# Whole projection tiles as 512 sample columns and 128 context columns, the context's halves in one product

## The chip, the cores and the metric

The kernel runs on one core of one Trainium2 chip. The time is device time in microseconds of one execution; 2773.0 us is the median of three runs of the kernel before (2765.32 to 2773.76). One profiled execution, 2764.28 us, gives the trace that is read here.

## The reference

One inference step of four layers, each a token mixer (windowed attention, spatial gating, short convolution, Fourier mixing) followed by a gated convolutional feed-forward part. 128 context tokens and 512 sample tokens go through the same weights. The dense products are nearly all of it:

```
def conv_ffn(h, w_up, conv_w, w_down):
    a = conv3_centred(h @ w_up, conv_w)
    g, u = a[..., :D_FF], a[..., D_FF:]
    return (jax.nn.silu(g) * u) @ w_down
```

with 1024 model columns and D_FF = 2816, in fp32. Before each sub-layer an RMS norm is modulated by shift and scale, and the result is added back through a gate, both from conditioning vectors (`c @ ada_w + ada_b`, other values for context and sample).

## The kernel before, in words

Activations lie with features on partitions and the 640 tokens on the free axis, the context's 128 first (`NP`, then `NS` = 512, `NT` = 640). To keep fp32 accuracy at the speed of fp32r, each operand is held as a high and a low part in fp32r, `[128, 4, 2, 640]` for activations (four feature blocks, high and low, tokens) and `[128, 2, 1024]` for a weight chunk. A product is then three: high x high, high x low, low x high (`mm3`, lines 489 to 491).

An output tile is 128 features x 640 tokens in a pair of PSUM banks (`new_pair`; the pool `pp` has three pairs). A bank holds 512 fp32, so the tile is done in two halves of 320 tokens, placed from column 192 (`PC0`) so that each half lies in one bank. For each k-step of 128 input features and each half, `pe_half` issues the three products: six products of 320 columns in a k-step.

`proj` runs over the output tiles of one weight matrix. A group of three tiles at the start (`lead`) is interleaved by a written plan, since its inputs are still being made; a group of three at the end (`tail`) lets the next norm start on the first half; the tiles between them are whole, one after the other. After a tile's products, `post` evacuates it, `ada.flush()` issues ACT's late accumulations, `W.pump` splits the next weight chunk (ACT casts the high part, L85; DVE, or POOL in places, subtracts for the low part, L86), and `ada.filler` issues one step of the modulation sums of a later layer: on DVE L208, on POOL L213, on ACT L214. The order of every engine is the order of the program.

In the feed-forward part the 44 up tiles of a layer go in three parts (16, 14, 14), each followed by the eight down tiles that sum into the residual (`PARTS`). In an up tile's `post`, ACT writes the middle tap (L612), DVE adds the outer taps for context and sample apart (L614 and L616, twice each), and the gate (L629 on ACT), the product (L636 on POOL, or L621 and L636 on DVE for the last two) and the split of the result (L589, L590) of the tiles before follow. The last three tiles of a part carry no step of the modulation (`quiet=3`). The down part begins with a lead of three tiles, one after the other over the first four k-steps, so it needs all three PSUM pairs; its residual add is L581.

Of the kernel before, what the change touches and what calls it, by code (L numbers as in the profile page):

```python
# [15 lines left out]
KT = 8  # L16
# [6 lines left out]
PC0 = 192  # L23
# [76 lines left out]
class Ada:  # L100
# [225 lines left out]
class Norm:  # L326
# [121 lines left out]

    def rhs(self, k, lo, hi):
        h = self.h[k // 4]  # L450
        return h[:, k % 4, 0, lo:hi], h[:, k % 4, 1, lo:hi]

# [41 lines left out]
def pe_half(g, ps, w, rhs, half, nk=KT, ks=None, at=None):  # L494
    out = ps[:, PC0 + OFF[half]:PC0 + OFF[half] + 320]
    for k in (range(nk) if ks is None else ks):
        rh, rl = rhs(k, OFF[half], OFF[half] + 320)
        c = slice(k * 128, (k + 1) * 128)
        mm3(g.nc, out, w[:, 0, c], w[:, 1, c], rh, rl, k == 0, k == nk - 1)
        if at and k in at:  # L500
            at[k]()


# [4 lines left out]
def proj(g, nm, M, rhs, post, nk=KT, lead=1, split=None, plan=None, hook=None, pre=None, tail=0, norm=None, rate=0.0, m0=0, quiet=0):  # L508
# [21 lines left out]
    while m < M - tail:  # L530
        if pre:
            w, ps = pre.pop(0)
        else:
            w, ps = W.take(), new_pair(g, f"{nm}{m0 + m}")
            pe_half(g, ps, w, rhs, 0, nk)
        for half in (1,):
            pe_half(g, ps, w, rhs, half, nk)
        post(m0 + m, ps, None)
        ada.flush()
        W.pump(g.wpool)  # L540
        ada.filler(rate if m < M - tail - quiet else 0.0)
        m += 1
# [30 lines left out]
def residual(g, l, i, norm=None):  # L573

    nc = g.nc

    def post(m, ps, half):
        lo, hi = (0, NT) if half is None else (OFF[half], OFF[half] + 320)
        gate = g.mod[:, l, i]
        for a, b, v in segs(lo, hi):  # L580
            nc.vector.scalar_tensor_tensor(out=g.x[:, m, a:b], in0=ps[:, PC0 + a:PC0 + b], scalar=gate[:, m, v:v + 1],  # L581
                                           in1=g.x[:, m, a:b], op0=ALU.mult, op1=ALU.add)
        if norm is not None:
            norm.add(m, half)
    return post
# [7 lines left out]
def ffn(g, l, norm, nxt):  # L593
# [10 lines left out]
    for p, (f0, nf) in enumerate(PARTS):  # L604
# [3 lines left out]
        def post(m, ps, half):  # L608
            f, isu = m // 2, m % 2
            col = (f + (NFF if isu else 0)) * 3  # L610
            c = g.tmp.tile([128, 640], F32, tag="tmp", name=f"c{l}_{m}")
            nc.scalar.activation(c, ps[:, PC0:PC0 + NT], AF.Copy, scale=fc[:, col + 1:col + 2])  # L612
            for a, b in ((0, NP), (NP, NT)):
                nc.vector.scalar_tensor_tensor(out=c[:, a + 1:b], in0=ps[:, PC0 + a:PC0 + b - 1], scalar=fc[:, col:col + 1],  # L614
                                               in1=c[:, a + 1:b], op0=ALU.mult, op1=ALU.add)
                nc.vector.scalar_tensor_tensor(out=c[:, a:b - 1], in0=ps[:, PC0 + a + 1:PC0 + b], scalar=fc[:, col + 2:col + 3],  # L616
                                               in1=c[:, a:b - 1], op0=ALU.mult, op1=ALU.add)
# [26 lines left out]

        def grhs(k, lo, hi):
            q = gq[k // 4]
            return q[:, k % 4, 0, lo:hi], q[:, k % 4, 1, lo:hi]

# [24 lines left out]
def attention(g, norm, nxt):  # L673
# [277 lines left out]
    proj(g, "wob", WA, orhs(1), residual(g, 0, 2, nxt), nk=4, rate=g.rate)  # L951
    proj(g, "wo", 3, lambda k, lo, hi: orhs(k // 4)(k % 4, lo, hi), residual(g, 0, 2, nxt), m0=WA, tail=3, norm=nxt, rate=0.0)


def sgu(g, norm, nxt):
# [5 lines left out]
    for q0 in range(0, 4, grp):  # L961
# [90 lines left out]
def shortconv(g, norm, nxt):  # L1052
# [46 lines left out]
def fnet(g, norm, nxt):  # L1099
# [77 lines left out]
def body(ctx, tc, io, depth=DEPTH):  # L1177
# [239 lines left out]
```

## Time and profile before

| what | value |
|---|---|
| median of three runs | 2773.0 us |
| profiled execution, and its span | 2764.28 us, 2762.5 us |
| TensorE products, busy | 2686.8 us, 97% of the span |
| weight loads, busy | 2613.8 us, 95% |
| DVE, ACT, POOL busy | 62%, 38%, 32% |
| DMA, mean | 107 GB/s |

How to read it: records of TensorE's products overlap, so their mean length (309 ns for 320 columns) is not their pace; the pace is read from start to start. DVE's share is a mean over stages that differ widely: in the first three layers' up projections it is near full, in the last layer's it is not.

### The profile page before, as it was taken

The numbers are of one execution on the slowest core, as the hardware profiler recorded it, in microseconds if no ns is written. First come the engines' busy times: TensorE is split into PE (matmuls) and PEld (weight loads), VectorE is DVE, ScalarE is ACT, GpSimd is POOL, SyncE is SP. The second block draws the span as 40 slices with busy tenths as digits, with TensorE's granted clock in tenths as the row PEclk, the third lists the DMA queues.
The fourth block names the chain that finished last, engine by engine and source line by source line (L and its number), as shares of the span: only waits on it lengthen the run. The fifth ranks groups of instructions, "written<-read, shape, count | busy, mean of one in ns | idle before, by whom it ended". The sixth has DMA issues, their size and how long they took to land.

```text
span 2762.5 us, 45506 instructions
## 1 busy us (share of the span) xinstructions
PE 2686.8 (97%) x18950; PEld 2613.8 (95%) x18950; DVE 1721.5 (62%) x2646; ACT 1043.7 (38%) x1672; POOL 878.3 (32%) x449
## 2 busy tenths in 40 slices
PE   8798899999999999999999999999999999999998
PEld 6676799999999999999999999999999999999998
DVE  6344687686964468586876335867678646434344
ACT  4344353343433245343444223534344424223232
POOL 1222153454520027354542001734354213111121
PEclk9999999999999999999999999999999999999999
DMA  6233333434322224333432221434343122221221
GB/s 255 79 100 114 116 128 119 145 131 144 140 75 73 73 81 158 122 136 125 152 107 71 77 77 55 160 115 140 121 153 126 47 69 78 69 83 63 84 70 45
DMA packets 88335, 295.35 MB, mean 107 GB/s; under 512 B 9665, under 2 KB 15553, under 8 KB 88129
## 3 DMA queue, kind: packets, MB, share of 16 engines
q1 hardware_dynamic: 87554, 292.19, 31.1%
q8 instruction: 149, 2.44, 0.3%
q14 instruction: 56, 0.46, 0.0%
q10 hardware_dynamic: 576, 0.26, 0.0%
HBM read 289.53 MB, written 2.88 MB: 106 GB/s over the span
## 4 chain that ended last, share of the span: by engine, by line
PE 85%; issue 7%; DVE 5%; ACT 2%; POOL 1%; DMA 1%; SPq 0%; POOLq 0%; DVEq 0%; ACTq 0%
PE up L489 15%; PE up L491 15%; PE up L490 15%; PE dn L489 6%; PE dn L491 6%; PE dn L490 6%; PE sc L489 2%; PE sc L490 2%; PE sc L491 2%; DVE t L417 1%; PE S L770 1%; PE O L849 1%; POOL w L86 1%; ACT w L85 1%; PE T L826 1%
## 5 line engine op out<-in xcount | busy, mean ns | idle before, releaser
L490 PE MATMUL up<-h,w 128*128 128x320 f32 x2816 | 871.2, 309 | 1.7 <-DVE h L429 1.7
L489 PE MATMUL up<-h,w 128*128 128x320 f32 x2816 | 872.1, 310 | 0.0
L491 PE MATMUL up<-h,w 128*128 128x320 f32 x2816 | 870.9, 309 | 0.0
L490 PEld LDWEIGHTS up<-h,w 128*128 128x128 f32 x2816 | 529.2, 188 | 3.1 <-DVE h L429 2.8
L489 PEld LDWEIGHTS up<-h,w 128*128 128x128 f32 x2816 | 529.2, 188 | 0.3
L491 PEld LDWEIGHTS up<-h,w 128*128 128x128 f32 x2816 | 529.1, 188 | 0.0
L86 DVE TENSOR_TENSOR w<-raw,w 128x1024 fp32r<-128x1024 f32 (+2 forms) x267 | 459.5, 1723 | 103.9 <-ACT w L85 96.1
L86 POOL TENSOR_TENSOR w<-raw,w 128x1024 fp32r<-128x1024 f32 (+2 forms) x94 | 218.6, 2326 | 796.1 <-ACT w L85 665.7
L213 POOL TENSOR_TENSOR adaq<-adaq,cb 128x1024 f32<-128x1024 f32 x138 | 349.7, 2534 | 360.0 <-ACT adaq L214 306.3
L85 ACT CAST w<-raw 128x1024 fp32r<-128x1024 f32 (+2 forms) x361 | 364.2, 1011 | 239.7 <-PE dn L491 162.2
L489 PE MATMUL dn<-g,w 128*128 128x320 f32 x1408 | 436.3, 310 | 0.0
L491 PE MATMUL dn<-g,w 128*128 128x320 f32 x1408 | 435.1, 309 | 0.0
L490 PE MATMUL dn<-g,w 128*128 128x320 f32 x1408 | 435.0, 309 | 0.0
L612 ACT ACTIVATE c<-up,fcv 128x640 f32<-128x640 f32 x176 | 140.1, 796 | 618.0 <-PE up L491 614.2
L614 DVE SCALAR_TENSOR_TENSOR c<-up,fcv,c 128x127 f32<-128x127 f32 x352 | 191.4, 544 | 251.3 <-ACT c L612 250.9
L490 PEld LDWEIGHTS dn<-g,w 128*128 128x128 f32 x1408 | 264.3, 188 | 0.3
L489 PEld LDWEIGHTS dn<-g,w 128*128 128x128 f32 x1408 | 264.3, 188 | 0.3
L491 PEld LDWEIGHTS dn<-g,w 128*128 128x128 f32 x1408 | 264.3, 188 | 0.0
L581 DVE SCALAR_TENSOR_TENSOR x<-dn,mod,x 128x128 f32<-128x128 f32 (+3 forms) x204 | 99.3, 526 | 250.5 <-PE dn L491 250.4
L208 DVE CUSTOM_DVE_ANT_0 adaq<-adaq,cb 128x1024 f32<-128x1024 f32 x138 | 254.5, 1844 | 0.1
L636 POOL TENSOR_TENSOR c<-c,c 128x640 f32<-128x640 f32 x64 | 150.1, 2345 | 180.0 <-DVE c L616 180.0
L616 DVE SCALAR_TENSOR_TENSOR c<-up,fcv,c 128x127 f32<-128x127 f32 x352 | 193.6, 550 | 12.4
(239 smaller groups left out, 3902.5 us busy)
## 6 DMA issues: line engine op xcount, KB each, us to landing
raw<-up SPq DMA_DIRECT2D x176, 512.0 KB, 3.7
adaq<-ada_t SPq DMA_DIRECT2D x138, 512.0 KB, 3.5
raw<-down SPq DMA_DIRECT2D x64, 448.0 KB, 3.6
adar<-ada SPq DMA_DIRECT2D x32, 512.0 KB, 3.5
raw<-down SPq DMA_DIRECT2D x32, 512.0 KB, 3.8
raw<-sc_in SPq DMA_DIRECT2D x24, 512.0 KB, 3.4
ada<-ada SPq DMA_DIRECT2D x16, 512.0 KB, 10.2
raw<-sgu_in SPq DMA_DIRECT2D x16, 512.0 KB, 3.6
```

Of the source, the lines that this page charges most:

```text
L85: nc.scalar.copy(w[:, 0, :n], raw[:, :n])
L86: (nc.gpsimd if pool else nc.vector).tensor_tensor(out=w[:, 1, :n], in0=raw[:, :n], in1=w[:, 0, :n], op=ALU.subtract)
L208: nc.vector.tensor_tensor_reduce(out=p0, in0=t, in1=g.cb[:, 0], scale=1.0, scalar=0.0, op0=ALU.mult, op1=ALU.add, accum_out=acc[:, 0:1])
L213: nc.gpsimd.tensor_tensor(out=p1, in0=t, in1=g.cb[:, 1], op=ALU.mult)
L489: nc.tensor.matmul(out, wh, rh, start=first, stop=False)
L490: nc.tensor.matmul(out, wh, rl, start=False, stop=False)
L491: nc.tensor.matmul(out, wl, rh, start=False, stop=last)
L581: nc.vector.scalar_tensor_tensor(out=g.x[:, m, a:b], in0=ps[:, PC0 + a:PC0 + b], scalar=gate[:, m, v:v + 1], in1=g.x[:, m, a:b], op0=ALU.m ...
L612: nc.scalar.activation(c, ps[:, PC0:PC0 + NT], AF.Copy, scale=fc[:, col + 1:col + 2])
L614: nc.vector.scalar_tensor_tensor(out=c[:, a + 1:b], in0=ps[:, PC0 + a:PC0 + b - 1], scalar=fc[:, col:col + 1], in1=c[:, a + 1:b], op0=ALU. ...
L616: nc.vector.scalar_tensor_tensor(out=c[:, a:b - 1], in0=ps[:, PC0 + a + 1:PC0 + b], scalar=fc[:, col + 2:col + 3], in1=c[:, a:b - 1], op0= ...
L636: eng.tensor_tensor(out=cg, in0=cg, in1=c, op=ALU.mult)
```

## The change

Whole tiles no longer go by halves. `pe_whole` computes, for each k-step, with the high weights the context's high and low parts side by side (one product of 256 columns, into columns 256 to 511 of the pair's first bank), then the sample's high and its low part (512 columns each, the second bank), and with the low weights the sample's high part (512) and the context's high part (128, onto columns 384 to 511). Columns 256 to 383 and 384 to 511 then each hold a part of the context's sum. After the last k-step ACT copies the first of them to a new small tile `ctx` (pool of two) and DVE adds it onto the second, in PSUM. The tile now starts at column 384, which the evacuations read through `g.pc`. Lead and tail tiles, and those that attention interleaves, stay as they were. The scratch output of the fused product and sum L147 moves from a tile of its own into the pool `tmp`.

```diff
+def pe_whole(g, ps, w, rhs, nk=KT):
+    PE = g.nc.tensor
+    for k in range(nk):
+        h = rhs(k)
+        wh, wl = w[:, 0, k * 128:(k + 1) * 128], w[:, 1, k * 128:(k + 1) * 128]
+        first, last = k == 0, k == nk - 1
+        PE.matmul(ps[:, 256:512], wh, h[:, :, 0:NP], start=first, stop=False)
+        PE.matmul(ps[:, 512:1024], wh, h[:, 0, NP:NT], start=first, stop=False)
+        PE.matmul(ps[:, 512:1024], wh, h[:, 1, NP:NT], start=False, stop=False)
+        PE.matmul(ps[:, 512:1024], wl, h[:, 0, NP:NT], start=False, stop=last)
+        PE.matmul(ps[:, 384:512], wl, h[:, 0, 0:NP], start=False, stop=last)
+    t = g.ctx.tile([128, NP], F32, tag="ctx", name="ctx")
+    g.nc.scalar.copy(t, ps[:, 256:384])
+    g.nc.vector.tensor_tensor(out=ps[:, 384:512], in0=ps[:, 384:512], in1=t, op=ALU.add)
...
     while m < M - tail:
         if pre:
             w, ps = pre.pop(0)
+            pe_half(g, ps, w, rhs, 1, nk)
         else:
             w, ps = W.take(), new_pair(g, f"{nm}{m0 + m}")
-            pe_half(g, ps, w, rhs, 0, nk)
-        for half in (1,):
-            pe_half(g, ps, w, rhs, half, nk)
+            pe_whole(g, ps, w, rhs, nk)
+            g.pc = 384
         post(m0 + m, ps, None)
+        g.pc = PC0
         ada.flush()
...
-            nc.scalar.activation(c, ps[:, PC0:PC0 + NT], AF.Copy, scale=fc[:, col + 1:col + 2])
+            nc.scalar.activation(c, ps[:, g.pc:g.pc + NT], AF.Copy, scale=fc[:, col + 1:col + 2])
...
-            V.tensor_tensor_reduce(out=t if v else g.junk, in0=t, in1=g.cb[:, v, c], scale=1.0, scalar=0.0, op0=ALU.mult, op1=ALU.add,
+            V.tensor_tensor_reduce(out=t if v else g.tmp.tile([128, 640], F32, tag="tmp", name=f"junk{self.pos}_{a}")[:, :512], in0=t, in1=g.cb[:, v, c], scale=1.0, scalar=0.0, op0=ALU.mult, op1=ALU.add,
```

Three places in the order of the engines, all at the tile `up_0_9` of the second layer's first part (`h` the normed activations, `w` the weight chunk). TensorE, the first k-steps of the tile, before:

```order
L489 MATMUL up_0_9_9958<-h_1_0_9207,w_9683 128x320
L490 MATMUL up_0_9_9958<-h_1_0_9207,w_9683 128x320
L491 MATMUL up_0_9_9958<-h_1_0_9207,w_9683 128x320
L489 MATMUL up_0_9_9958<-h_1_0_9207,w_9683 128x320
L490 MATMUL up_0_9_9958<-h_1_0_9207,w_9683 128x320
L491 MATMUL up_0_9_9958<-h_1_0_9207,w_9683 128x320
```

and now, from the last product of the tile ahead:

```order
L515 MATMUL up_0_8_9552<-h_1_1_8894,w_9297 128x128
L511 MATMUL up_0_9_9614<-h_1_0_8893,w_9359 128x256
L512 MATMUL up_0_9_9614<-h_1_0_8893,w_9359 128x512
L513 MATMUL up_0_9_9614<-h_1_0_8893,w_9359 128x512
L514 MATMUL up_0_9_9614<-h_1_0_8893,w_9359 128x512
L515 MATMUL up_0_9_9614<-h_1_0_8893,w_9359 128x128
```

Five products stand for six, and a 128-column one stands ahead of each k-step's first. DVE around the same tile, before (`c` is the convolved tile, `adaq` the modulation's block):

```order
L208 ISA adaq_9291,part<-adaq_9291,cb 128x1024
L208 ISA part 128x1
L614 SCALAR_TENSOR_TENSOR c_9_10007<-up_0_9_9958,fcv_9292,c_9_10007 128x127
L616 SCALAR_TENSOR_TENSOR c_9_10007<-up_0_9_9958,fcv_9292,c_9_10007 128x127
L614 SCALAR_TENSOR_TENSOR c_9_10007<-up_0_9_9958,fcv_9292,c_9_10007 128x511
L616 SCALAR_TENSOR_TENSOR c_9_10007<-up_0_9_9958,fcv_9292,c_9_10007 128x511
L86 TENSOR_TENSOR w_10015<-raw_9886,w_10015 128x1024
```

and now (L614 and L616 have become L632 and L634):

```order
L208 ISA adaq_8977,part<-adaq_8977,cb 128x1024
L208 ISA part 128x1
L518 TENSOR_TENSOR up_0_9_9614<-up_0_9_9614,ctx 128x128
L632 SCALAR_TENSOR_TENSOR c_9_9658<-up_0_9_9614,fcv_8978,c_9_9658 128x127
L634 SCALAR_TENSOR_TENSOR c_9_9658<-up_0_9_9614,fcv_8978,c_9_9658 128x127
L632 SCALAR_TENSOR_TENSOR c_9_9658<-up_0_9_9614,fcv_8978,c_9_9658 128x511
L634 SCALAR_TENSOR_TENSOR c_9_9658<-up_0_9_9614,fcv_8978,c_9_9658 128x511
L86 TENSOR_TENSOR w_9666<-raw_9547,w_9666 128x1024
```

The add stands between the step of the tile ahead and this tile's taps. ACT at the same tile, now (L612, the middle tap, has become L630):

```order
L85 CAST w_9606<-raw_9484 128x1024
L517 COPY ctx<-up_0_9_9614 128x128
L630 ACTIVATE c_9_9658<-up_0_9_9614,fcv_8978 128x640
L647 ACTIVATE c_8_9596<-c_8_9596 128x640
L214 ACTIVATE adaq_8977,part<-adaq_8977 128x1024
```

The copy is new, ahead of the middle tap, which reads what the add has written.

## Rows read from the trace of the kernel before

**Rows 1.** The page: busy us of the engines, share of the span, instructions

```profile
PE 2686.8 (97%) x18950; PEld 2613.8 (95%) x18950; DVE 1721.5 (62%) x2646; ACT 1043.7 (38%) x1672; POOL 878.3 (32%) x449
```

**Rows 2.** Timeline, TensorE, up projection (start, length, engine, line, tiles, shapes)

```profile
1086.49 0.31 PE L489 MATMUL up<-h,w 128*128 128x320 f32 x1
...
1114.79 0.31 PE L490 MATMUL up<-h,w 128*128 128x320 f32 x1
```

**Rows 3.** Timeline, TensorE, sgu's value projection

```profile
869.98 0.28 PE L489 MATMUL sv<-w,h 128*128 128x256 f32 x1
...
877.90 0.28 PE L489 MATMUL sv<-w,h 128*128 128x256 f32 x1
```

**Rows 4.** Timeline, TensorE, Fourier mixer

```profile
2218.50 0.39 PE L490 MATMUL f<-dftM,U 128*128 128x512 f32 x1
...
2220.77 0.39 PE L491 MATMUL f<-dftM,U 128*128 128x512 f32 x1
```

**Rows 5.** Timeline, loads and products behind six one-column products, attention's output projection

```profile
341.96 0.19 PEld L489 LDWEIGHTS wo<-O,w 128*128 128x128 f32 x1
341.98 0.39 PE L489 MATMUL wo<-O,w 128*128 128x320 f32 x1
342.07 0.19 PEld L490 LDWEIGHTS wo<-O,w 128*128 128x128 f32 x1
...
342.21 0.31 PE L490 MATMUL wo<-O,w 128*128 128x320 f32 x1
```

**Rows 6.** Windows, up projection (length; PE, PEld, DVE, ACT, POOL busy; clock; DMA)

```profile
1050.00:1120.00 70.00, 70.00 (x479) 70.00 (x479) 62.99 (x73) 33.21 (x49) 37.74 (x18) 1.00 0.39 137
```

**Rows 7.** Timeline, DVE, two step tiles of the same up projection

```profile
1080.55 0.35 DVE L614 SCALAR_TENSOR_TENSOR c<-up,fcv,c 128x127 f32<-128x127 f32 x1
...
1081.97 0.75 DVE L616 SCALAR_TENSOR_TENSOR c<-up,fcv,c 128x511 f32<-128x511 f32 x1
...
1085.60 2.60 DVE L208 CUSTOM_DVE_ANT_0 adaq<-adaq,cb 128x1024 f32<-128x1024 f32 x1
1088.13 0.08 DVE L208 DVE_READ_ACCUMULATOR2_ANT part<- 128x1 f32 x1
...
1090.21 3.02 DVE L86 TENSOR_TENSOR w<-raw,w 128x1024 fp32r<-128x1024 f32 x1
1093.15 1.21 DVE L208 CUSTOM_DVE_ANT_0 adaq<-adaq,cb 128x1024 f32<-128x1024 f32 x1
1094.30 0.08 DVE L208 DVE_READ_ACCUMULATOR2_ANT part<- 128x1 f32 x1
```

**Rows 8.** Timeline, ACT, the middle taps of these tiles

```profile
1079.65 0.80 ACT L612 ACTIVATE c<-up,fcv 128x640 f32<-128x640 f32 x1 [3.64 <-PE up L491]
...
1086.69 0.80 ACT L612 ACTIVATE c<-up,fcv 128x640 f32<-128x640 f32 x1 [3.64 <-PE up L491]
```

**Rows 9.** Timeline, POOL, the same tiles

```profile
1084.56 2.56 POOL L636 TENSOR_TENSOR c<-c,c 128x640 f32<-128x640 f32 x1
...
1089.73 2.42 POOL L213 TENSOR_TENSOR adaq<-adaq,cb 128x1024 f32<-128x1024 f32 x1
```

**Rows 10.** Timeline, DVE, the last tiles of the part, without a step

```profile
1111.24 1.23 DVE L86 TENSOR_TENSOR w<-raw,w 128x1024 fp32r<-128x1024 f32 x1 [0.36 <-ACT w L85]
1115.74 0.35 DVE L614 SCALAR_TENSOR_TENSOR c<-up,fcv,c 128x127 f32<-128x127 f32 x1 [3.28 <-ACT c L612]
...
1120.39 1.23 DVE L86 TENSOR_TENSOR w<-raw,w 128x1024 fp32r<-128x1024 f32 x1
```

**Rows 11.** Timelines, DVE and TensorE, the third down tile behind the last up tile

```profile
1124.21 0.75 DVE L616 SCALAR_TENSOR_TENSOR c<-up,fcv,c 128x511 f32<-128x511 f32 x1
...
1125.21 0.31 PE L489 MATMUL dn<-g,w 128*128 128x320 f32 x1
```

**Rows 12.** Timeline, TensorE, an idle time (in brackets), and the window behind it

```profile
324.39 0.61 PE L489 MATMUL wo<-O,w 128*128 128x320 f32 x1 [2.83 <-DVE x L581]
...
324.13:327.54 3.41, 3.15 (x12) 3.18 (x13) 2.41 (x4) 1.67 (x2) 0.00 (x0) 0.50 0.46 159
```

More of the change, by code (lines that the diff above doesn't have):

```diff
@@ L447, in drain, with rhs @@
             self.low = None
-    def rhs(self, k, lo, hi):
-        h = self.h[k // 4]
-        return h[:, k % 4, 0, lo:hi], h[:, k % 4, 1, lo:hi]
+    def rhs(self, k):
+        return self.h[k // 4][:, k % 4]
     def hook(self, half, k):
@@ L496, in pe_half @@
     for k in (range(nk) if ks is None else ks):
-        rh, rl = rhs(k, OFF[half], OFF[half] + 320)
+        h = rhs(k)[:, :, OFF[half]:OFF[half] + 320]
         c = slice(k * 128, (k + 1) * 128)
-        mm3(g.nc, out, w[:, 0, c], w[:, 1, c], rh, rl, k == 0, k == nk - 1)
+        mm3(g.nc, out, w[:, 0, c], w[:, 1, c], h[:, 0], h[:, 1], k == 0, k == nk - 1)
         if at and k in at:
             at[k]()
+def pe_whole(g, ps, w, rhs, nk=KT):
[12 more added lines that the diff above has]
+    g.nc.vector.tensor_tensor(out=ps[:, 384:512], in0=ps[:, 384:512], in1=t, op=ALU.add)
 def new_pair(g, nm):
@@ L580, in post @@
         for a, b, v in segs(lo, hi):
-            nc.vector.scalar_tensor_tensor(out=g.x[:, m, a:b], in0=ps[:, PC0 + a:PC0 + b], scalar=gate[:, m, v:v + 1],
+            nc.vector.scalar_tensor_tensor(out=g.x[:, m, a:b], in0=ps[:, g.pc + a:g.pc + b], scalar=gate[:, m, v:v + 1],
                                            in1=g.x[:, m, a:b], op0=ALU.mult, op1=ALU.add)
@@ L611, in post @@
             c = g.tmp.tile([128, 640], F32, tag="tmp", name=f"c{l}_{m}")
[L612 removed]
+            nc.scalar.activation(c, ps[:, g.pc:g.pc + NT], AF.Copy, scale=fc[:, col + 1:col + 2])
             for a, b in ((0, NP), (NP, NT)):
[L614 removed]
+                nc.vector.scalar_tensor_tensor(out=c[:, a + 1:b], in0=ps[:, g.pc + a:g.pc + b - 1], scalar=fc[:, col:col + 1],
                                                in1=c[:, a + 1:b], op0=ALU.mult, op1=ALU.add)
[L616 removed]
+                nc.vector.scalar_tensor_tensor(out=c[:, a:b - 1], in0=ps[:, g.pc + a + 1:g.pc + b], scalar=fc[:, col + 2:col + 3],
                                                in1=c[:, a:b - 1], op0=ALU.mult, op1=ALU.add)
@@ L643, in ffn, with grhs @@
         flush()
-        def grhs(k, lo, hi):
-            q = gq[k // 4]
-            return q[:, k % 4, 0, lo:hi], q[:, k % 4, 1, lo:hi]
+        def grhs(k):
+            return gq[k // 4][:, k % 4]
         last = p == len(PARTS) - 1
@@ L724, in post @@
             t = g.tmp.tile([128, 640], F32, tag="tmp", name=f"q{j}")
-            A.copy(t[:, 128:640], ps[:, PC0 + 128:PC0 + 640])
-            A.copy(at.qst[:, j, :128], ps[:, PC0:PC0 + 128])
+            A.copy(t[:, 128:640], ps[:, g.pc + 128:g.pc + 640])
+            A.copy(at.qst[:, j, :128], ps[:, g.pc:g.pc + 128])
             rope_S([(at.qst[:, j, 128:640], 0, 512)], t, f"q{j}")
@@ L729, in post @@
             t = g.tmp.tile([128, 640], F32, tag="tmp", name=f"k{j}")
-            A.copy(t, ps[:, PC0:PC0 + NT])
+            A.copy(t, ps[:, g.pc:g.pc + NT])
             A.dma_start(out=io["new_k"][:, j, :], in_=t[:, :128])
@@ L735, in post @@
             t = g.tmp.tile([128, 640], F32, tag="tmp", name=f"v{j}")
-            A.copy(t, ps[:, PC0:PC0 + NT])
+            A.copy(t, ps[:, g.pc:g.pc + NT])
             A.dma_start(out=io["new_v"][:, j, :], in_=t[:, :128])
@@ L882, in orhs @@
     def orhs(gp):
-        return lambda k, lo, hi: (at.O[gp][:, k, 0, lo:hi], at.O[gp][:, k, 1, lo:hi])
+        return lambda k: at.O[gp][:, k]
     WA = KT - 3
@@ L971, in vmm @@
         def vmm(i, tc, k):
-            hh, hl = norm.rhs(k, tc * 128, (tc + 1) * 128)
+            h = norm.rhs(k)[:, :, tc * 128:(tc + 1) * 128]
+            hh, hl = h[:, 0], h[:, 1]
             w = ws[i][k // 4]
@@ L1044, in sgu, with rhs @@
     proj(g, "su", KT, norm.rhs, post, rate=g.srate)
-    def rhs(k, lo, hi):
-        return oq[k // 4][:, k % 4, 0, lo:hi], oq[k // 4][:, k % 4, 1, lo:hi]
+    def rhs(k):
+        return oq[k // 4][:, k % 4]
     out_proj(g, "sgo", 1, rhs, nxt, lead=3, plan=late_plan(KT, 4), split=0)
@@ L1059, in post @@
         j, kind = m // 3, m % 3
-        pv = ps[:, PC0:PC0 + NT]
+        pv = ps[:, g.pc:g.pc + NT]
         if kind == 0:
@@ L1167, in fnet, with rhs @@
             stage2(k - 1)
-    def rhs(k, lo, hi):
-        return oq[k // 4][:, k % 4, 0, lo:hi], oq[k // 4][:, k % 4, 1, lo:hi]
+    def rhs(k):
+        return oq[k // 4][:, k % 4]
     g.W.cap = len(g.W.chunks)
@@ L1189, in body @@
     g.fcv = pool("fcv", 1)
+    g.ctx = pool("ctx", 2)
     g.quad = pool("quad", 5)
@@ L1231, in body @@
     g.wpool = False
+    g.pc = PC0
     g.rate, g.urate, g.drate, g.srate, g.mix = 1.0, 1.0, 1.0, 0.0, 1
```

9 lines of the change are left out of this document (4 added, 5 removed).

## The prediction

> **What bounds the kernel now.** I read the page first: TensorE is busy 97% of the span and its weight loads 95%, DVE 62% [rows 1]. A busy share of overlapping records is not a pace, so the second view is the timeline of TensorE alone, in stretches without a wait, from start to start. In an up projection 193 starts lie between 1086.49 and 1114.79 us: 146.6 ns for each 320-column product [rows 2]. The sgu products of 256 columns follow each other at 7.92 us / 66 = 120.0 ns [rows 3], those of 512 columns in the Fourier mixer at 2.27 us / 10 = 227 ns [rows 4]. All three lie on one line: 0.4167 ns a column (the 2.4 GHz level) and about 13.3 ns for each product. The reader is to see that columns cost nearly everything, and that one product less is worth 13 ns at most.
>
> The third view is TensorE's loads beside its products where a product is short [rows 5]. Six one-column products stand just ahead. The load for L489 is issued at 341.96, the next load only at 342.07, and L490's product at 342.21, 0.14 to 0.15 after that: in the steady rows a load is issued when the product before it really begins, so L489's product, recorded at 341.98, began at about 342.07. One fp32r load of 128 columns needs 0.11 us and only one is held ahead. Under a 320-column product it is hidden; under a short one it is not.
>
> The fourth view is DVE in the same up stretch. Over 70 us TensorE is never idle, and DVE is busy 62.99 [rows 6]. In a tile that carries a step of the modulation sums (L208) DVE has no room: its L208 ends at 1088.21, 1.5 us after the next tile's L612 began on ACT [rows 7, 8]. So there are two limits here, one almost on top of the other.
>
> **The change part by part.** *Products.* A k-step had six products of 320 columns, now 256, three of 512, and 128: 1920 columns either way, one product less. Whole tiles are: qkv 3, wob 5 (four k-steps each), su 8, the three output projections 2 each, sc 21, up 41 a layer, dn 12 a layer (5 of 8 k-steps, 7 of 7). k-steps: 24 + 20 + 64 + 48 + 168 + 1312 + 356 = 1992, in 255 tiles. The order of TensorE has 1992 rows less.
>
> Before, a k-step takes 6 x 146.6 = 880 ns. After: 120 + 3 x 227 + X, where X is the time from the 128-column product to the next one's start. No row shows such a product in fp32r. From below, the line of rows 2 to 4 gives 53 + 13 = 67 ns, if its successor's load is hidden; from above 111 + 13 = 124 ns, if the fixed part adds to the load. I take 111 ns, the load of rows 5, which is the nearest: a load of the same type behind a product shorter than itself. Then the k-step is 120 + 681 + 111 = 912 ns, 32 ns more, and 1992 x 32 = **+63 us**; the ends are -24 and +89 us. A tile of eight k-steps goes from 7.04 to 7.29 us. Only the last product of a k-step is too short; the 256-column one ahead is not, since 120 ns cover a load.
>
> The Trainium skill has a rule against this choice: "TensorE: Matmul & The Clock Gate", section on weight-path perf modes, says that a fast weight load is on for 128 weights of any type but FP32. By it the load would be hidden, X would be 67 ns and this term -24 us. Rows 5 speak against it for fp32r.
>
> *The sum of the halves.* Each whole tile gains a copy on ACT and an add on DVE, both 128x128 and out of PSUM, ahead of the tile's evacuation. The nearest row for the add is L614's 128x127 with one operand in PSUM, 0.35 us [rows 7]; the copy I put at the same. 255 x 0.35 = 89 us for each engine beside TensorE, which would be free if they were idle. In the up projections the position matters more than the length. ACT's L612 reads the sum, so it now waits for DVE's add, and the add stands in DVE's queue behind the last tile's L86 and L208. Before, L612 ran while DVE was still at that L208: it starts at 1086.69 and DVE ends at 1088.21 [rows 7, 8]. Now DVE does the add, waits for L612 (0.80), then does L614 and L616. Queued behind that waiting instruction are L86 (the low halves of weights taken five tiles later, so no hurry), L208, and the next tile's add, for whose tile three PSUM pairs wait.
>
> Work of a step tile on DVE, from L612's end to the end of L208's read: 1080.45 to 1088.21 = 7.76, and 1087.49 to 1094.38 = 6.89, mean 7.32 us [rows 7, 8]. It is that long because L86 and L208, 1.23 and 1.21 us when alone, take 3.02 and 2.60 when POOL's L213 or L636 runs [rows 7, 9, 10]; POOL's steps hang on ACT's chain, which starts with L612 too, so I expect the same meetings. With 0.35 for the add, 0.80 for L612 and about 0.1 for the two hand-overs the cycle is 7.32 + 1.25 = **8.57 us** against TensorE's 7.29. DVE falls back 1.28 us a tile.
>
> A part has 10 or 11 step tiles: 11 x 1.28 = 14.1 us behind. The last three tiles carry no step. The first of them takes DVE 0.10 + 2.17 (L614 to L616, 1080.55 to 1082.72) + 0.36 + 1.23 [rows 7, 10] + 1.25 = 5.1 and gives 2.2 back; the next carries a product for g as well, 0.1 + 5.88 (1115.74 to 1121.62) + 1.25 = 7.2 [rows 10] and gives 0.1. So the last tile is evacuated 14.1 - 2.3 = 11.8 us later than it would be by its own chain, which is itself 0.8 us longer (copy 0.35, add 0.35, hand-overs). The down projection begins with three tiles in the three PSUM pairs. Before, the last up tile's L616 ends at 1124.96, and the third down tile takes that pair at 1125.21: 0.25 us in hand [rows 11]. The stall at the end of a part is therefore 11.8 + 0.8 - 0.25 = 12.3 us, less about 1 that TensorE has waited before, when DVE is over two tiles behind: **11 us**. Parts with steps are three in each of the first three layers (138 of L208 in all; the last layer has none): 9 x 11 = **+99 us**. From below it is 0, if POOL and DVE meet less often (L86 and L208 at 1.2 each give a cycle of 6.3, under 7.29); from above 20 a part, +180. I take the value that the rows of step tiles give.
>
> *What such a stall does to the clock.* Behind an idle time of 2.83 us on TensorE the granted clock is 0.50, the 1.2 GHz level, for 3.41 us [rows 12]; that costs 1.7 us of work. At one such window a part: 9 x 1.7 = **+15 us** (0 to 31).
>
> *Small ones.* The last layer's three parts end 0.8 - 0.25 = 0.6 us late: +2. In wob a tile is short (four k-steps), and right behind it TensorE waits for DVE's L581 [rows 12], so five adds and their hand-overs count in full: 5 x 0.45 = +2 to +4, I take 3. The scratch output of L147 moves into the tmp pool, in and around wob alone: nothing, since nobody reads it and DVE frees it in its own order. The other renamed slices move no instruction. DMAs stay as they are.
>
> The sum, against the profiled execution's 2764.3 us (span 2762.5): 2764.3 + 63 + 99 + 15 + 5 = 2946. The median of the runs, 2773.0, is 9 above this execution; I forecast **2950 us**.
>
> **Rivals.** *DVE keeps up, only the load counts*: 2764 + 63 + 9 = 2836. For it: the waits for POOL may fall apart when the phases move; against it: rows 7 and 8 have no slack for 1.25 us. *The load hides, DVE lags*: a tile of 8 x 867 ns = 6.93 us lets DVE fall back 1.64 a tile, 18 us by the end, a stall of about 16 in nine parts; 2764 - 24 + 146 + 15 + 5 = 2906. *The load hides and DVE keeps up*: the other side; its place is the step from the 128-column product to the next k-step's first, its price 13 ns won on each of 1992, less some 5 us of small ones; 2764 - 24 + 5 = 2745. It decides as soon as X is under 80 ns. Rows 2 to 4 are for the 67 ns, rows 5 against. *X near 80 ns and no lag*: the k-step is 881 ns, no change, 2764 + 2 + 5 = 2771.
> The same page of the Trainium skill gives, in its section on the back-to-back issue gap, 81 ns for a sustained stream of 128-column products with their loads; that is the last rival, and no run here shows it.
>
> **How the numbers follow.** Forecast 0.57 (its own range 2895 to 3000), load alone 0.21, DVE alone 0.08, neither 0.08, near 80 ns 0.04, worse than 3000 0.02. The range 2825 to 3000 takes in the first three but for their edges, some 0.82. About 0.3% (8 us) is what a measurement of this kernel can tell from no change. Faster 0.08, same 0.04, slower 0.88.
>
> **What would show it.** In the changed kernel's timeline of TensorE: from the 128-column product to the next start 0.11 us (0.067 would refute the first term), 0.227 and 0.12 for the others. In DVE's rows of an up tile: the wait for ACT's middle tap, now in every step tile, 0.8 to 0.9 us, and a cycle above 8 us. In TensorE's waits: dn behind DVE at the end of nine parts, some 10 us each, with a half clock behind it, and none in the last layer. If DVE's cycle in step tiles stays at TensorE's pace and dn doesn't wait, the second term is wrong; if a k-step is 867 ns the first is, and the sign may be too.

## The result, and the profile after

The changed kernel takes **2947.0 us** (median of 4 runs, 2945.1 to 2950.8) against 2772.9 of the kernel before on the same chip: ratio 1.0636 [1.0614, 1.0658], 174 us slower. The forecast was 2950, the range 2825 to 3000.

The profiled execution has a span of 2943.2 us at a mean clock of 0.981; before it was 2762.5 at 0.993. The page's busy line and its chain shares:

```profile
PE 2805.8 (95%) x16958; PEld 2464.9 (84%) x16958; DVE 1806.7 (61%) x2901; ACT 1096.6 (37%) x1927; POOL 858.2 (29%) x449
...
PE 54%; DVE 22%; ACT 12%; issue 9%; POOL 1%; DMA 1%; DVEq 0%; POOLq 0%; SPq 0%; ACTq 0%
```

Against [rows 1] TensorE has 1992 products and loads less, and DVE and ACT 255 instructions more each. No engine's share rose. What rose is the part of DVE in the chain that ends last, to 22% (the page of before has 5%), although DVE is busy 61% as before: a busy share does not show that an engine has become a bound.

**TensorE in a k-step.** The timeline of the weight loads in the last layer's up projection (start, length, engine, line, tiles, shapes), the rows that answer to [rows 2 to 5]:

```profile
2651.52 0.19 PEld L515 LDWEIGHTS up<-h,w 128*128 128x128 f32 x1
2651.75 0.19 PEld L511 LDWEIGHTS up<-h,w 128*128 128x128 f32 x1
2651.86 0.19 PEld L512 LDWEIGHTS up<-h,w 128*128 128x128 f32 x1
2651.98 0.19 PEld L513 LDWEIGHTS up<-h,w 128*128 128x128 f32 x1
2652.21 0.19 PEld L514 LDWEIGHTS up<-h,w 128*128 128x128 f32 x1
2652.45 0.19 PEld L515 LDWEIGHTS up<-h,w 128*128 128x128 f32 x1
```

and of the products, the 128-column one and the next:

```profile
2651.75 0.22 PE L515 MATMUL up<-h,w 128*128 128x128 f32 x1
2651.81 0.33 PE L511 MATMUL up<-h,w 128*128 128x256 f32 x1
```

Read the loads and not the products. A load is issued when the product before it really begins, so from L511's load (2651.75) to L512's (2651.86) is the time of the 128-column product: 0.11 us, as in [rows 5]. The products' own records put L511 0.06 behind L515; by the loads that is too early, since its weights are not there yet. Over some 1300 k-steps of up the mean intervals of the load issues are 108.4 (128 columns), 121.1 (256), 232.0, 233.1 and 230.0 ns (the three of 512): 924.6 ns a k-step, against 880.

**DVE in a step tile**, the second layer's first part, the rows that answer to [rows 7], and the two middle taps on ACT, to [rows 8] (in brackets the idle time ahead and what ended it):

```profile
1114.25 0.29 DVE L518 TENSOR_TENSOR up<-up,ctx 128x128 f32<-128x128 f32 x1
1115.47 0.35 DVE L632 SCALAR_TENSOR_TENSOR c<-up,fcv,c 128x127 f32<-128x127 f32 x1 [0.93 <-ACT c L630]
...
1118.00 2.58 DVE L86 TENSOR_TENSOR w<-raw,w 128x1024 fp32r<-128x1024 f32 x1 [0.35 <-ACT w L85]
1120.50 2.59 DVE L208 CUSTOM_DVE_ANT_0 adaq<-adaq,cb 128x1024 f32<-128x1024 f32 x1
...
1123.02 0.29 DVE L518 TENSOR_TENSOR up<-up,ctx 128x128 f32<-128x128 f32 x1
1124.24 0.35 DVE L632 SCALAR_TENSOR_TENSOR c<-up,fcv,c 128x127 f32<-128x127 f32 x1 [0.93 <-ACT c L630]
```

```profile
1114.57 0.80 ACT L630 ACTIVATE c<-up,fcv 128x640 f32<-128x640 f32 x1 [3.02 <-DVE up L518]
...
1118.62 0.27 ACT L517 COPY ctx<-up 128x128 f32<-128x128 f32 x1 [0.65 <-PE up L515]
1123.35 0.79 ACT L630 ACTIVATE c<-up,fcv 128x640 f32<-128x640 f32 x1 [4.46 <-DVE up L518]
```

TensorE is done with the tile at 1118.6 (the copy starts), and its middle tap runs at 1123.35, since the add stands behind L86 and L208 of the tile ahead. In [rows 8] the middle tap waited for TensorE alone. Over the 96 tiles with a step, from the end of one tile's taps to the end of the next one's, DVE takes 8.27 us against TensorE's tile of 7.40, so it falls back. Before it took 6.98 us, which is TensorE's pace there (a tile of 7.04) and not DVE's own need.

**Where it ends.** The waits of ACT and DVE in the up tiles, and TensorE's longest (us in total, times, longest):

```profile
ACT c L630 <- DVE up L518: 427.4, 164, 5.7
...
DVE c L632 <- ACT c L630: 162.8, 172, 2.1
...
PE dn L488 <- DVE c L634: 59.7, 21, 5.1
```

One part's end, the second and third down tile of the second layer, on TensorE's timeline:

```profile
1189.63 0.38 PE L488 MATMUL dn<-g,w 128*128 128x320 f32 x1 [2.68 <-DVE c L634]
1196.64 0.61 PE L488 MATMUL dn<-g,w 128*128 128x320 f32 x1 [4.74 <-DVE c L634]
```

and the window behind the first of them (length; busy of PE, PEld, DVE, ACT, POOL; clock; DMA share, GB/s):

```profile
1191.10:1201.34 10.24, 5.50 (x22) 5.13 (x21) 7.15 (x10) 4.08 (x6) 0.00 (x0) 0.50 0.15 51
```

Before, dn waited for no tap ([rows 11] has 0.25 us in hand). Now nine parts wait, 59 us in all, and the last layer's three only 0.4 each. Behind the nine the clock is at its 1.2 GHz level for 61 us altogether. Against the run without the sum below, which has the same products, the nine dn stages are 84 us longer: the 59 of waits, and 25 for the half clock. So the 181 us of span are 89 in the k-steps, 59 in waits at dn, 25 in the half clock, and some 8 elsewhere.

### The profile page after: what moved, and what is told of

Its sections match the earlier page's. It is cut to its first block, busy times and chain, and to the rows that moved or that the text cites. A ratio compares the mean times of both kernels' runs of the same rounds, so it can differ in the third digit from the quotient of the medians.

```text
span 2943.2 us, 42029 instructions
## 1 busy us (share of the span) xinstructions
PE 2805.8 (95%) x16958; PEld 2464.9 (84%) x16958; DVE 1806.7 (61%) x2901; ACT 1096.6 (37%) x1927; POOL 858.2 (29%) x449
## 4 chain that ended last, share of the span: by engine, by line
PE 54%; DVE 22%; ACT 12%; issue 9%; POOL 1%; DMA 1%; DVEq 0%; POOLq 0%; SPq 0%; ACTq 0%
DVE w L86 8%; DVE adaq L208 5%; ACT w L85 4%; PE up L513 3%; PE up L512 3%; PE up L514 3%; ACT adaq L214 3%; ACT c L630 3%; PE dn L488 3%; PE up L511 3%; PE dn L513 2%; PE dn L512 2%; PE dn L489 2%; PE dn L514 2%; PE dn L490 2%
## 5 line engine op out<-in xcount | busy, mean ns | idle before, releaser
L86 DVE TENSOR_TENSOR w<-raw,w 128x1024 fp32r<-128x1024 f32 (+2 forms) x267 | 491.0, 1841 | 106.2 <-ACT w L85 91.6
L513 PE MATMUL up<-h,w 128*128 128x512 f32 x1312 | 518.4, 395 | 0.0
L512 PE MATMUL up<-h,w 128*128 128x512 f32 x1312 | 517.4, 394 | 0.0
L514 PE MATMUL up<-h,w 128*128 128x512 f32 x1312 | 513.9, 392 | 0.0
L213 POOL TENSOR_TENSOR adaq<-adaq,cb 128x1024 f32<-128x1024 f32 x138 | 334.5, 2424 | 429.3 <-ACT adaq L214 384.9
L86 POOL TENSOR_TENSOR w<-raw,w 128x1024 fp32r<-128x1024 f32 (+2 forms) x94 | 217.5, 2315 | 817.8 <-ACT w L85 685.9
L511 PE MATMUL up<-h,w 128*128 128x256 f32 x1312 | 437.2, 333 | 1.3 <-DVE c L634 1.2
L85 ACT CAST w<-raw 128x1024 fp32r<-128x1024 f32 (+2 forms) x361 | 363.9, 1010 | 108.4 <-PE dn L490 107.6
L630 ACT ACTIVATE c<-up,fcv 128x640 f32<-128x640 f32 x176 | 139.9, 795 | 431.1 <-DVE up L518 427.4
L515 PEld LDWEIGHTS up<-h,w 128*128 128x128 f32 x1312 | 246.4, 188 | 59.4
L514 PEld LDWEIGHTS up<-h,w 128*128 128x128 f32 x1312 | 246.4, 188 | 57.2
L511 PEld LDWEIGHTS up<-h,w 128*128 128x128 f32 x1312 | 246.3, 188 | 56.8 <-ACT adaq L214 1.4
L632 DVE SCALAR_TENSOR_TENSOR c<-up,fcv,c 128x127 f32<-128x127 f32 x352 | 192.0, 545 | 162.8 <-ACT c L630 162.8
L515 PE MATMUL up<-h,w 128*128 128x128 f32 x1312 | 290.2, 221 | 0.0
L488 PE MATMUL dn<-g,w 128*128 128x320 f32 x696 | 228.9, 329 | 59.9 <-DVE c L634 59.7
L512 PEld LDWEIGHTS up<-h,w 128*128 128x128 f32 x1312 | 251.1, 191 | 0.0
L513 PEld LDWEIGHTS up<-h,w 128*128 128x128 f32 x1312 | 247.1, 188 | 0.0
L208 DVE CUSTOM_DVE_ANT_0 adaq<-adaq,cb 128x1024 f32<-128x1024 f32 x138 | 225.8, 1636 | 0.1
L489 PE MATMUL dn<-g,w 128*128 128x320 f32 x696 | 224.1, 322 | 0.0
L490 PE MATMUL dn<-g,w 128*128 128x320 f32 x696 | 223.4, 321 | 0.0
L634 DVE SCALAR_TENSOR_TENSOR c<-up,fcv,c 128x127 f32<-128x127 f32 x352 | 193.6, 550 | 12.4
```

The costliest lines, as they stand in the source:

```text
L85: nc.scalar.copy(w[:, 0, :n], raw[:, :n])
L86: (nc.gpsimd if pool else nc.vector).tensor_tensor(out=w[:, 1, :n], in0=raw[:, :n], in1=w[:, 0, :n], op=ALU.subtract)
L208: nc.vector.tensor_tensor_reduce(out=p0, in0=t, in1=g.cb[:, 0], scale=1.0, scalar=0.0, op0=ALU.mult, op1=ALU.add, accum_out=acc[:, 0:1])
L213: nc.gpsimd.tensor_tensor(out=p1, in0=t, in1=g.cb[:, 1], op=ALU.mult)
L488: nc.tensor.matmul(out, wh, rh, start=first, stop=False)
L489: nc.tensor.matmul(out, wh, rl, start=False, stop=False)
```

## The experiments

Theory: two costs, TensorE's dearer k-step and DVE's lag behind the sum, and the second comes from the place of the add and not from its length. Rivals: TensorE alone; the sum's length; the load hidden.

| kernel | us | ratio to before |
|---|---|---|
| changed, no sum | 2861.6 | 1.0337 [1.0322, 1.0353] |
| before, with a dummy sum | 2910.7 | 1.0517 [1.0499, 1.0534] |
| changed, low product 256 wide | 2956.6 | 1.0681 [1.0663, 1.0699] |
| changed, short product twice | 3101.6 | 1.1204 [1.1188, 1.1221] |
| before, dummy sum aside | 2909.7 | 1.0503 [1.0489, 1.0518] |
| before, dummy sum behind the tap | 2777.8 | 1.0042 [1.0026, 1.0058] |
| changed, step in the wait | 2918.2 | 1.0536 [1.0523, 1.0550] |
| changed, tap apart | 2870.0 | 1.0370 [1.0356, 1.0384] |
| split 384 and 256 | 2908.4 | 1.0498 [1.0482, 1.0514] |
| the same where no step runs | 2769.3 | 0.9996 [0.9987, 1.0006] |
| and the last layer's up | 2764.3 | 0.9984 [0.9974, 0.9994] |

**1. Each cost alone.** The changed kernel without the sum:

```diff
-    t = g.ctx.tile([128, NP], F32, tag="ctx", name="ctx")
-    g.nc.scalar.copy(t, ps[:, 256:384])
-    g.nc.vector.tensor_tensor(out=ps[:, 384:512], in0=ps[:, 384:512], in1=t, op=ALU.add)
```

> The changed kernel without the copy on ACT and the add on DVE; so the product of the high weights and the context's low part is left out of the result. My theory: two costs, TensorE's k-step (925 ns in the changed kernel's rows against 880, 1992 of them, +89 us) and DVE's lag behind the sum. Without the sum only the first stays: 2773 + 89 = 2862 us (2852 to 2872), a tile of eight k-steps still 7.40 us, no wait of dn for DVE of over 1 us and no half clock behind it, and DVE's wait for ACT's middle tap gone from the step tiles. Rival, TensorE alone (the waits at dn come from longer tiles or later weights, not from the sum): the waits stay, 2947 us.

Measured 2861.6 us, 93 more than before; no wait of dn for a tap is left, and DVE's cycle in a step tile is 7.35 us, TensorE's pace. That is the k-steps' price; TensorE alone does not explain the other 85. And the kernel before, with a sum that changes no value:

```diff
+        t = g.ctx.tile([128, NP], F32, tag="ctx", name="ctx")
+        g.nc.scalar.copy(t, ps[:, PC0:PC0 + NP])
+        g.nc.vector.tensor_tensor(out=ps[:, PC0:PC0 + NP], in0=ps[:, PC0:PC0 + NP], in1=t, op=ALU.max)
         post(m0 + m, ps, None)
```

> The kernel before, its six products of 320 columns as they were, with a copy on ACT of the 128 context columns and a DVE operation on the same columns in each whole tile ahead of the evacuation (the maximum of the value and its own copy, so nothing is changed by it): the second cost without the first. My theory: a tile stays 7.04 us, DVE's cycle in a step tile goes to about 8.4, DVE falls back 1.3 to 1.4 us in each of 11 tiles, and dn waits some 12 us at the end of nine parts, with half a clock behind it: 2773 + 9 x 14 + 5 = 2905 us (2880 to 2925). Rival, DVE's lag needs the longer products or the sum is hidden: 2773 to 2780 us.

This kernel and the two of part 3 also carry the change of L147's scratch output. Measured 2910.7 us: the sum alone costs 142. Its waits:

```profile
ACT c L615 <- DVE up L540: 449.3, 164, 5.7
...
PE dn L489 <- DVE c L619: 69.3, 29, 5.0
...
PE up L489 <- DVE c L619: 20.5, 21, 1.6
```

DVE's cycle is 8.27 us here too, but against a tile of 7.04, so that TensorE waits within up already. The two costs do not add: 93 and 142 alone, 174 together, because the dearer k-step gives DVE 0.36 us more a tile.

**2. Where the k-step's 45 ns come from.** Two kernels change the short product; a third has none.

```diff
-        PE.matmul(ps[:, 384:512], wl, h[:, 0, 0:NP], start=False, stop=last)
+        PE.matmul(ps[:, 256:512], wl, h[:, :, 0:NP], start=False, stop=last)
```

> The changed kernel with its last product of a k-step 256 columns wide instead of 128 (low weights by the context's high and low part); the product of the two low parts is added to the result. It puts the question where the 45 ns of a k-step come from. A: 512 columns take 227 ns as in my sum and the 128-column product takes 125, the load and the fixed part one after the other: then the k-step is 2 x 120 + 3 x 227 = 921 ns, 4 less than now, and the time is 2947 - 8 = 2939 us. B: the 128-column product takes 111 as I put it, and 512 columns take 232 here: 2 x 120 + 3 x 232 = 936 ns, 11 more, +22 us, and DVE falls back 0.09 us less a tile, 9 parts of 11 tiles, -9: 2960 us. C, the load is hidden and the 128-column product takes 67: then it adds 53 ns, +106 us, less some 40 of lag: 3010 us.

Measured 2956.6 us, between A and B. The means of the load issues say why: the two 256-column products take 116 and 117.5 ns, and 512 columns 235, 231 and 227.5, a k-step of 927. C is out; of A and B it is B, with 256 columns 3 ns cheaper than I put them. The k-steps explain 5 of the 10 us. The mean granted clock is lower too, 0.978 against 0.981 over four runs each, some 7 to 9 us by an estimate from these two; why it is lower isn't settled.

```diff
+        PE.matmul(ps[:, 384:512], wl, h[:, 0, 0:NP], start=False, stop=False)
         PE.matmul(ps[:, 384:512], wl, h[:, 0, 0:NP], start=False, stop=last)
```

> The changed kernel with its 128-column product issued twice, one right behind the other (the product of the low weights and the context's high part counts double in the result). It measures the short product by itself: 1992 more of them. Exposed load, 111 to 125 ns each: a k-step of 1036 (B) to 1050 (A) ns, a tile of 8.29 to 8.40 us, which is DVE's own cycle, so the waits at dn all but go, some -75 us: 2947 + 221 - 75 = 3093 us (B) to 2947 + 249 - 75 = 3121 us (A). Hidden load, 67 ns each: a tile of 7.94 us, the waits about halve: 2947 + 133 - 40 = 3040 us.

Measured 3101.6 us, nearest to B. The loads in up, with L515 and L516 the two short products:

```profile
2651.08 0.19 PEld L516 LDWEIGHTS up<-h,w 128*128 128x128 f32 x1
2651.19 0.19 PEld L511 LDWEIGHTS up<-h,w 128*128 128x128 f32 x1
2651.30 0.19 PEld L512 LDWEIGHTS up<-h,w 128*128 128x128 f32 x1
2651.42 0.19 PEld L513 LDWEIGHTS up<-h,w 128*128 128x128 f32 x1
2651.66 0.19 PEld L514 LDWEIGHTS up<-h,w 128*128 128x128 f32 x1
```

L516's load to L511's and L511's to L512's are the two short products: 0.11 us each. The whole k-step, 1040 ns, is 115 longer than in the changed kernel, and that does not hang on which record is read. With a tile of 8.32 us DVE keeps up, and the waits at dn are 5.2 us in all, without a half clock. A rival would be that 128 columns take 0.11 us by themselves. [rows 5] speak against it: the last of the six products there is one column wide, and from L489's load to L490's it is 0.11 us as well. So a product of 128 columns costs its successor's load and not its columns.

The third has five products and none shorter than a load:

```diff
+        PE.matmul(ps[:, 128:512], wh, h[:, 0, 0:384], start=first, stop=False)
+        PE.matmul(ps[:, 128:512], wh, h[:, 1, 0:384], start=False, stop=False)
+        PE.matmul(ps[:, 128:512], wl, h[:, 0, 0:384], start=False, stop=last)
+        PE.matmul(ps[:, 512:1024], wh, h[:, :, 384:NT], start=first, stop=False)
+        PE.matmul(ps[:, 512:768], wl, h[:, 0, 384:NT], start=False, stop=last)
...
+    g.nc.scalar.copy(t, ps[:, 768:1024])
+    g.nc.vector.tensor_tensor(out=ps[:, 512:768], in0=ps[:, 512:768], in1=t, op=ALU.add)
```

> The changed kernel with the other split that has five products in a k-step: the context and the first 256 other tokens together (three products of 384 columns), the last 256 tokens' high and low parts side by side (512 columns) and their low weights by 256 columns. Nothing is left out. No product is shorter than a load; the sum is 256 columns wide. My theory: 384 columns take 173 ns by the line of the kernel before, 512 take 231 and 256 take 117 as the rows of the changed kernel and its two variants have it, so a k-step is 3 x 173 + 231 + 117 = 868 ns, 12 under the kernel before, 1992 x -12 = -24 us. The add goes to 0.44 us and the copy to 0.36, DVE's cycle to 8.65 us against a tile of 6.94, and it falls back 1.7 us a tile: 11 x 1.7 - 2 = 16.5 us and a half clock's 1.7 at the end of nine parts, +164. In all 2768 - 24 + 164 + 5 = 2913 us (2890 to 2940). If five products cost more than six whatever their widths, the k-step is over 880 ns and the time is over 2940 us.

Measured 2908.4 us. The loads in up (L511 to L513 the 384-column products, L514 the 512, L515 the 256; an interval tells of the product before its first line):

```profile
2651.48 0.19 PEld L515 LDWEIGHTS up<-h,w 128*128 128x128 f32 x1
2651.70 0.19 PEld L511 LDWEIGHTS up<-h,w 128*128 128x128 f32 x1
2651.82 0.19 PEld L512 LDWEIGHTS up<-h,w 128*128 128x128 f32 x1
2652.00 0.19 PEld L513 LDWEIGHTS up<-h,w 128*128 128x128 f32 x1
2652.17 0.19 PEld L514 LDWEIGHTS up<-h,w 128*128 128x128 f32 x1
```

On the mean of all of up 384 columns take 173.9 ns, 512 take 229.3 and 256 take 116.7: 868 ns, 13 under the kernel before (881 measured the same way). The products gain; the sum takes it back: TensorE waits for the taps 74.5 us at dn and 39.2 within up.

**3. Place or length of the add.** The dummy sum, with an output that nobody reads:

```diff
-        g.nc.vector.tensor_tensor(out=ps[:, PC0:PC0 + NP], in0=ps[:, PC0:PC0 + NP], in1=t, op=ALU.max)
+        g.nc.vector.tensor_tensor(out=t, in0=ps[:, PC0:PC0 + NP], in1=t, op=ALU.max)
```

> The kernel before with the same copy on ACT and the same DVE operation in each whole tile as in the run with halves and a dummy sum (2910.7 us), but its output goes into the copy's tile and nobody reads it, so ACT's middle tap no longer waits for DVE. The two operations stay, the hand-over between them and the taps goes. My theory, the position is the price and not the length: DVE's own time grows by 0.29 us a tile, and it had 0.7 us idle in a tile of 7.04 (62.99 of 70 busy): 2768 to 2800 us, I take 2780. Rival, the length of the two operations is the price: about 2910 us.

Measured 2909.7 us, as the rival has it, but the run did not take the wait away. ACT's timeline:

```profile
1108.63 0.79 ACT L615 ACTIVATE c<-up,fcv 128x640 f32<-128x640 f32 x1 [4.14 <-DVE ctx L540]
```

In this program ACT's read of the PSUM tile stays behind DVE's, though both only read. So the operation was moved behind the tap:

```diff
+        def aside(t=t, ps=ps):
+            g.nc.vector.tensor_tensor(out=t, in0=ps[:, PC0:PC0 + NP], in1=t, op=ALU.max)
...
             nc.scalar.activation(c, ps[:, PC0:PC0 + NT], AF.Copy, scale=fc[:, col + 1:col + 2])
+            if g.mid:
+                g.mid()
```

> The kernel before with the same copy on ACT and the same unread DVE operation as in the run with the sum aside (2909.7 us), but in the up projections the DVE operation is issued behind ACT's middle tap. In the run with the sum aside, ACT's L615 still began only after DVE's L540 (4.14 and 5.24 us idle, then 0.3 us behind it), though both only read the tile: so that run took nothing of the wait away and told length and position apart not at all. Here ACT's tap waits for no DVE work of its tile. Position is the price: 0.29 us of DVE in a tile of 7.04, of which 0.7 were idle, 2768 to 2800 us, I take 2785. Length is the price: about 2910 us.

Measured 2777.8 us: the same two operations cost 9 us instead of 141. DVE's rows of one tile:

```profile
1108.52 2.60 DVE L208 CUSTOM_DVE_ANT_0 adaq<-adaq,cb 128x1024 f32<-128x1024 f32 x1
...
1111.05 0.28 DVE L541 TENSOR_TENSOR ctx<-up,ctx 128x128 f32<-128x128 f32 x1
1111.25 0.34 DVE L625 SCALAR_TENSOR_TENSOR c<-up,fcv,c 128x127 f32<-128x127 f32 x1
```

The taps follow at once, and the cycle is 6.98 us as before. The place is the price.

**4. Two ways to mend the wait.** First, the step of the modulation is issued behind the add, so that L208 runs while ACT does the middle tap:

```diff
+            g.mid = lambda: ada.filler(rate if m < M - tail - quiet else 0.0)
+            post(m0 + m, ps, None)
...
             nc.scalar.activation(c, ps[:, g.pc:g.pc + NT], AF.Copy, scale=fc[:, col + 1:col + 2])
+            if g.mid:
+                g.mid()
```

(The add stands ahead of `post`, in `pe_whole`; ACT's late accumulation of a tile's step, once issued behind the next tile's `post`, now comes with the next step.)

> The changed kernel with DVE's step of the modulation sums issued between the add and the taps of the same tile, in the up projections alone, so that it stands in the queue where DVE waits for ACT's middle tap. Nothing is left out. My theory: of the sum's price the 0.93 us that DVE waits for ACT (its rows at 1115.47 and 1124.24) is the larger part and the add's own 0.29 the smaller. Covered by L208, the cycle in a step tile goes from 8.4 us to about 7.5 against TensorE's 7.40, DVE falls back 0.1 us a tile instead of 1.0, and nearly all of the 85 us of waits goes: 2947 - 75 = 2872 us (2860 to 2890). Rival, the sum costs by its length or by what it does to POOL's and ACT's meetings with DVE: DVE still falls back, 2920 to 2947 us.

Measured 2918.2 us: 29 of the 85 gone, not 75. Another wait took its place, on POOL, ACT and DVE:

```profile
1166.64 1.56 POOL L662 TENSOR_TENSOR c<-c,c 128x640 f32<-128x640 f32 x1
...
1168.23 0.73 ACT L613 CAST g<-c 128x640 fp32r<-128x640 f32 x1 [4.02 <-POOL c L662]
...
1169.94 1.75 DVE L86 TENSOR_TENSOR w<-raw,w 128x1024 fp32r<-128x1024 f32 x1 [4.38 <-ACT w L85]
```

The step's POOL part now comes ahead of POOL's product for g; ACT's cast waits for that product, ACT's L85 stands behind the cast, and DVE's L86 behind L85. Two tiles take 15.1 us together here, 4.4 of them this wait for L85; over the step tiles DVE's mean cycle is 7.9 us, still above TensorE's 7.40.

Second, the middle tap is divided: ACT does the sample's 512 columns ahead of the add, DVE the context's 128 behind it.

```diff
+                nc.scalar.activation(c[:, NP:NT], ps[:, g.pc + NP:g.pc + NT], AF.Copy, scale=fc[:, col + 1:col + 2])
+                g.mid()
...
+                nc.vector.tensor_scalar(out=c[:, 0:NP], in0=ps[:, g.pc:g.pc + NP], scalar1=fc[:, col + 1:col + 2], scalar2=None, op0=ALU.mult)
```

(`g.mid` holds the add).

> The changed kernel, its products, copy and add as they are, but in the up projections ACT's middle tap takes the 512 other columns alone and ahead of the add, and the context's 128 columns of it are computed by DVE right behind the add. Nothing is left out. DVE no longer waits for ACT in a step tile (0.93 us) and has one more operation of 128 columns (0.29): its cycle goes from 8.4 us to 7.5 to 7.8 against TensorE's 7.40, and the waits at dn fall to 0 to 3 us a part: the products' 2862 us and 0 to 25, I take 2875 us (2862 to 2895). If the wait is not the price but the add's length, or what the later start of L86 and L208 does to their meetings with POOL, it stays over 2920 us.

Measured 2870.0 us. DVE's rows:

```profile
1107.28 0.29 DVE L519 TENSOR_TENSOR up<-up,ctx 128x128 f32<-128x128 f32 x1
1107.67 0.35 DVE L639 TENSOR_SCALAR c<-up,fcv 128x128 f32<-128x128 f32 x1
1108.06 0.35 DVE L643 SCALAR_TENSOR_TENSOR c<-up,fcv,c 128x127 f32<-128x127 f32 x1
...
1110.15 2.30 DVE L86 TENSOR_TENSOR w<-raw,w 128x1024 fp32r<-128x1024 f32 x1
```

One more operation on DVE, and 77 us less: the cycle is 7.35 us, and dn waits 6.9 us in all. Of the 102 us that are left over before, 93 are the k-steps' price as in the run without the sum.

**5. A version that could beat both:** the split 384 and 256 where DVE carries no step, halves elsewhere.

```diff
+            if nk < 7 or nm in ("qkv", "wob") or (nm[:2] == "up" and rate > 0):
+                pe_half(g, ps, w, rhs, 0, nk)
+                pe_half(g, ps, w, rhs, 1, nk)
+            else:
+                pe_whole(g, ps, w, rhs, nk)
```

> The split in 384 and 256 only where DVE has room: the last layer's up tiles, the down projections, the spatial and the convolution mixer's and the output projections (964 of 1992 k-steps); the up tiles of the first three layers, qkv and wob keep the halves of the kernel before. My theory: 964 x -12 ns = -12 us, the sum hidden but for about 1 us at the end of the last layer's three parts: 2768 - 12 + 3 = 2759 us, some 0.3% faster than the kernel before. Rival, the sum costs in the other projections too (behind residual sums and norms): 2768 us or more.

Measured 2769.3 us, no change. My count was off: the last layer's loop has a rate too, so it kept its halves, and 636 k-steps changed and not 964. The stages with them are shorter by 0.2 to 0.8 us each (the convolution mixer's by 0.6, where its 168 k-steps should give 2.2), but half clocks behind waits of other stages gave as much back (mean clock 0.988 against 0.993 in the two profiles, and 0.988 against 0.991 over all runs). With the last layer's up tiles too:

```diff
-            if nk < 7 or nm in ("qkv", "wob") or (nm[:2] == "up" and rate > 0):
+            if nk < 7 or nm in ("qkv", "wob") or (nm[:2] == "up" and (nm[2] != "3" or m >= M - 3)):
```

> As the run with the split in 384 and 256 only where DVE has room (2769.3 us), and the last layer's up tiles too, but for the last three of each part, so that no sum stands in front of dn: 32 tiles, 256 k-steps more at -13.3 ns (866.7 against 880), -3.4 us. In that earlier run the last layer had kept its halves, since its loop carries a rate of steps though no step is left: 636 k-steps, -8.5 us, and its profile gives +8.7 back in longer half clocks (behind the waits of sv, two starts of up and the Fourier mixer). If these are chance: 2769 - 8.5 - 3.4 = 2757 us. If the shorter stretches bring them each time: 2766 us, which is no change to the kernel before.

Measured 2764.3 us, 0.16% under before, and the interval does not reach 1: of the 12 us that the products should give, 4 are won and two thirds lost. The half clocks do not look like chance: this profile has them where the last one had them (in sv, at the start of the second layer's up, in the convolution mixer), and the mean clock over its runs is 0.988 again. How the shorter stages would bring them stays open.

## Why the prediction was right

The case that I held likeliest came, by its own steps. Three terms were mis-sized, two too low and one too high, and nearly cancel: that the forecast is only 3 us off is luck.

| term | predicted | measured |
|---|---|---|
| products, 1992 k-steps | +63 | +89 (93 without the sum) |
| waits at dn, nine parts | +99 | +59 |
| half clock behind them | +15 | +25 |
| small ones | +5 | about +8 |

*Products.* The disputed step was right: 111 ns for the 128-column product, 108 measured; the load is exposed. The rule of the Trainium skill ("TensorE: Matmul & The Clock Gate", weight-path perf modes), that a fast load is on for 128 weights of any type but FP32, would hide it only if fp32r counts as another type than FP32; the 108 ns speak against that reading. What failed is "3 x 227", and it brings the term to the upper end that I gave: I took it from ten products of [rows 4], and it is 230 to 233 here. 14 ns more for three, 3 less for the short one, 1 more for the 256: 924.6 against 912. The mixer's 96 products of 512 columns have medians of 227, 231 and 236 ns by line in the trace of before, and the ten that I took lie at the lower end.

*The lag.* "The position matters more than the length" was right (9 us of length against 142 in all). The cycle of 8.57 us is 8.27, and both of its terms were a little too long: over the 96 step tiles the changed kernel takes 7.19 us from the middle tap's end to the end of L208's read where I had 7.32, and 1.08 for the add, the tap and the hand-overs where I had 1.25 (the add is 0.29 and not 0.35). With TensorE's tile at 7.40 and not 7.29, DVE falls back 0.87 us a tile and not 1.28. The rest of my sum for the end of a part, as it stands, makes 6.8 us of that; 6.5 are waited in a part, where I had 11. That a dearer k-step makes the lag cheaper was in the working (the tile is in the subtraction), but the two terms were sized apart; the dummy sum shows how much hangs on it.

*The clock.* One stretch of 3.41 us at 1.2 GHz a part was too little: there are 61 us in nine parts. dn waits twice in each of them, at its second and third tile, and behind the two lie, in eight of the nine, two such stretches or a longer one.

*Rivals.* Load alone is the run without the sum: 2862, where I had 2836 with 227 for 512 columns. That the load hides, or that X is near 80 ns, is refuted by the 108, and with it the side on which the change would have won. That the wait at dn all but goes in the last layer, where no step runs, came as said: 0.4 us a part.

## What to carry to other kernels

Cutting a product so that one piece is shorter than a weight load does not save the product's fixed part but pays for the load; cut so that every piece covers one. An operation put between PSUM and its evacuation costs by whose queue it stands in and who waits behind it: look for the instruction that now waits on another engine, and move that, before counting lengths. Where two engines are near the same pace, a cost on the one is cover for the other, so test each alone and both together. Take a pace from all rows of the stage that is changed, and not from ten of another.

## What was not expected of the hardware

Products of 256, 320 and 384 columns lie near one line (116 to 121, 146.6 and 173.9 ns), but 512 columns take 231 to 233.5 on the mean of the three in a k-step (single positions 227.5 to 235.7), where that line has 227. Two times 256 side by side as one product take 229.3. Why is not settled.
